# The first product of three of four MLP blocks as seven half-size products, with the masks loaded once per mixer

## The chip, the core and the metric

The kernel runs on one core of one Trainium2 chip. TensorE multiplies, VectorE (DVE), ScalarE (ACT) and GpSimd (POOL) work element by element, and SyncE (SP) issues nearly all transfers between the chip's memory and the core. The metric is the device time of one execution in microseconds (us); less is better.

## What is computed

The reference runs one step of a two-layer decoder. Each layer has a mixer (recurrent heads, different in layer 0 and layer 1) and an MLP, both followed by a layer norm:

```python
h = _layer_norm(ALPHA * h + mixed, p['ln1_g'][layer], p['ln1_b'][layer])
h = _layer_norm(ALPHA * h + _sq_relu_mlp(h, p['mlp_w1'][layer], p['mlp_w2'][layer]), ...)

def _sq_relu_mlp(h, w1, w2):
    return jnp.square(jax.nn.relu(h @ w1)) @ w2
```

There are 592 tokens (576 in the last MLP), the width is 1024 and the MLP is 4096 wide. All is fp32.

## The kernel before

Activations lie with the features on the 128 partitions and the tokens along the row: `H` is eight tiles of 128 features by 592 tokens. Every fp32 operand of a product is kept as two fp32r parts, a rounded copy made by ACT and the rest made by DVE (`split`, `parts`), and a product is three matmuls, high by high, high by low and low by high. The weights come as 252 units of 128 by 1024 through three `raw` buffers. `parts` splits a unit with one ACT cast (L126) and one DVE subtraction (L127) into one of five `w` buffers. A conventional tile (`mm`, L182) takes eight k-steps of three matmuls for each half of the tokens, so two tiles cost 96 matmuls of 296 tokens (288 in the last MLP).

The MLP works in four blocks of 1024 features. For a block the first product, w1, gives eight tiles; relu and square follow on ACT, and DVE and ACT split the squares into operands. The second product, w2, adds eight tiles into the running sums `r`. For three of the four blocks (`FAST`) w2 runs as pairs of tiles, and a pair takes seven products of half size in place of eight (`fast_pair`, `product` L195): four k-steps by three matmuls by seven are 84 matmuls. For that, DVE forms sums and differences of weights (L141, L142, L148, L149) and of squares (L632 to L638), and three and a half unit splits take the place of two. w1 is conventional in all four blocks, and so is w2 in the last one.

At the head of both mixers stands a small product with 16 columns of weights (`wsr`, 32 columns with the two parts; `mm32` L247 and `together` L311). Its weights for both layers are loaded and split once, while the input x arrives (L356 to L358). A table of masks (`msk`, 561 KB) is loaded once as well (L362). After layer 0 the output of the MLP is stored to memory for the residual of layer 1: eight times a POOL addition (L682) and a store issued by POOL (L683). These are the last things that read the `r` tiles.

The order of the instructions on each engine is fixed when the program is built. A scheduler takes the code in the order in which it is written and moves instructions past each other by costs of its own; where a buffer is taken over from an earlier tile, it puts in waits for all that used that tile. An engine then runs its list in order.

Of the kernel before, what the change touches and what calls it, by code (L numbers as in the profile page):

```python
# [14 lines left out]
P = 128  # L15
# [56 lines left out]
def _trunk(ctx, tc, nc, I, O):  # L72
# [20 lines left out]
    msk = const.tile([P, NMSK], F32, name="msk")  # L93
# [3 lines left out]
    onesr = const.tile([P, P], F32R, name="onesr")  # L97
# [5 lines left out]
    def mk(name):  # L103
        a, b = MSK[name]
        return msk[:, a:b]

    ident, umask, lsmask, uxmask, lxmask, seqm, sel, blk = (
        mk(n) for n in ("ident", "u", "ls", "ux", "lx", "seq", "sel", "blk"))
# [95 lines left out]
    def fast_pair(xs, n, y11, y12, y21, y22):  # L204
# [5 lines left out]
        def add(y, p):  # L210
            V.tensor_tensor(y, y, p[:, :n], OP.add)  # L211

        def sub(y, p):
            V.tensor_tensor(y, y, p[:, :n], OP.subtract)
# [4 lines left out]
        add(y11, X)  # L219
        product(W, u1, HD, xs["b21"], n, True)  # L220
        add(y11, W)
        flush()
        prep_to(base + 5)
        product(Z, u3, HD, xs["t1"], n, True)
        sub(y22, Z)
# [3 lines left out]
        add(y12, X)  # L229
        product(Z, u2, HD, xs["b22"], n, False)  # L230
        add(y12, Z)
# [3 lines left out]
        sub(y22, X)  # L235

        def rest():
            product(X, u4, 0, xs["t4"], n, False)
            sub(y21, X)
# [106 lines left out]
    with ExitStack() as st:  # L346
# [15 lines left out]
    nc.sync.dma_start(msk, I["msk"])  # L362
    nc.sync.dma_start(row, I["row"])
    G.memset(ones, 1.0)
    A.copy(onesr, ones)
# [218 lines left out]
    def mlp(H, layer, halves, last, keep=None):  # L584

        n = halves[0][1] - halves[0][0]
        c0, c1 = halves[0][0], halves[1][1]
        with ExitStack() as st:
            rp = pool("mr", KT, stack=st)
            tp = pool("mt", 1, stack=st)  # L590
            fp = pool("mf", 5, stack=st)
            rs = [rp.tile([P, T], F32, tag="r", name="r") for _ in range(KT)]
            ff, stage, made = {}, {}, {}
            out = [None]
            scratch = []

            def new(name):
                if not scratch:
                    scratch.append(fp.tile([P, 7, T], F32, tag="ff", name="ln"))
                    scratch.append(0)  # L600
                scratch[1] += 1
                return scratch[0][:, scratch[1] - 1]
# [926 lines left out]
def layout(inp):  # L1529
# [32 lines left out]
    def mlp_units(l):  # L1562
# [6 lines left out]
        for b in range(4):  # L1569
            if b < 3:  # L1570
                u += a(b + 1, 0, 2)
# [104 lines left out]
```

## Time and profile before

| | |
|---|---|
| time, median of three runs | 1898.5 us (1894.89 to 1899.44) |
| the profiled execution's own time | 1896.57 us |
| its span in the trace | 1894.8 us |
| TensorE (PE) busy | 1842.8 us, 97% of the span |
| DVE busy | 1258.0 us, 66% |
| ACT busy | 942.3 us, 50% |
| POOL busy | 363.4 us, 19% |

The trace gives each instruction's start and duration. On DVE and ACT the end of an instruction overlaps the start of the next, so what one costs in a full queue is the distance between two starts. The view of stretches gives for each engine how long it was busy between two times and PEclk, the share of TensorE's full clock that was granted: 1.00 is 2.4 GHz and 0.50 is 1.2 GHz. PE is the row of matmuls and PEld the row of weight loads beside it. Names are the program's tiles with the buffer numbers left out, and an arrow points from inputs to output.

### The profile page before, as it was taken

What the parts mean: (1) busy time and instruction counts of PE and PEld (TensorE: products, weight loads), DVE (VectorE), ACT (ScalarE), POOL (GpSimd) and SP (SyncE); (2) the same over time, 40 slices, a digit from 0 to 9 for tenths busy, and PEclk for the clock granted to TensorE, in tenths of its full rate; (3) what the DMA queues carried; (4) which work ended last, traced back from release to release, by engine and by line L of the source; (5) the groups of instructions that cost most, each with busy time, mean ns of one, the idle gap of its engine ahead of it and who ended that gap; (6) DMA issues with size and microseconds to landing.
All of it is one profiled execution on the core that took longest, in us unless ns stands there. A gap on an engine that the chain in (4) does not pass through costs nothing.

```text
span 1894.8 us, 33652 instructions
## 1 busy us (share of the span) xinstructions
PE 1842.8 (97%) x13822; PEld 1802.8 (95%) x13822; DVE 1258.0 (66%) x2003; ACT 942.3 (50%) x1718; POOL 363.4 (19%) x403
## 2 busy tenths in 40 slices
PE   8999999998999999998999999999999899999996
PEld 8998999998999999997999999999999899999996
DVE  7776757759875757458754565665755976666638
ACT  6656456624744443324644455666632653534333
POOL 2122324015000000145322121221203200000015
PEclk9999999999999999999999999999999999999998
DMA  6232221321222232313323233223231214141411
GB/s 220 91 115 72 88 101 68 114 84 56 67 80 99 67 112 68 120 59 113 113 96 114 104 103 104 80 99 106 82 128 57 78 57 134 45 134 45 134 57 50
DMA packets 68761, 175.96 MB, mean 93 GB/s; under 512 B 6624, under 2 KB 30304, under 8 KB 67456
## 3 DMA queue, kind: packets, MB, share of 16 engines
q1 hardware_dynamic: 67968, 171.40, 26.9%
q8 instruction: 108, 1.77, 0.4%
q0 software_dynamic: 640, 2.43, 0.3%
q14 instruction: 45, 0.37, 0.1%
HBM read 154.54 MB, written 19.25 MB: 92 GB/s over the span
## 4 chain that ended last, share of the span: by engine, by line
PE 81%; DVE 13%; ACT 3%; issue 2%; POOL 0%; DMA 0%; ACTq 0%; DVEq 0%
PE pm L182 54%; PE pm L195 14%; PE pm L311 2%; DVE w L127 2%; DVE r L515 1%; DVE r L531 1%; DVE h L533 1%; DVE r L451 1%; PE px L1375 1%; DVE acc L748 1%; PE px L1386 1%; PE px L1385 1%; PE px L1118 1%; ACT w L126 1%; PE px L1314 1%
## 5 line engine op out<-in xcount | busy, mean ns | idle before, releaser
L182 PE MATMUL pm<-h,w 128*128 128x296 f32 (+2 forms) x7728 | 1102.1, 301 | 6.2 <-ACT h L334 5.6
L182 PEld LDWEIGHTS pm<-h,w 128*128 128x128 f32 x7728 | 1057.6, 189 | 16.1 <-ACT h L334 5.6
L127 DVE TENSOR_TENSOR w<-raw,w 128x1024 fp32r<-128x1024 f32 (+1 forms) x300 | 367.3, 1225 | 199.0 <-ACT w L126 197.8
L126 ACT CAST w<-raw 128x1024 fp32r<-128x1024 f32 (+1 forms) x300 | 304.1, 1014 | 293.2 <-PE pm L195 153.1
L195 PE MATMUL pm<-ff,w 128*128 128x296 f32 (+1 forms) x2016 | 273.3, 297 | 0.0
L195 PEld LDWEIGHTS pm<-ff,w 128*128 128x128 f32 x2016 | 272.0, 188 | 0.0
L657 POOL TENSOR_TENSOR sq<-sq 128x296 f32<-128x296 f32 (+1 forms) x32 | 21.5, 674 | 652.4 <-ACT sq L655 652.4
L182 PE MATMUL pm<-m,w 128*128 128x296 f32 (+1 forms) x768 | 105.1, 298 | 0.0
L182 PE MATMUL pm<-ff,w 128*128 128x296 f32 (+1 forms) x768 | 105.0, 298 | 0.0
L182 PEld LDWEIGHTS pm<-m,w 128*128 128x128 f32 x768 | 103.8, 188 | 0.4
L182 PEld LDWEIGHTS pm<-ff,w 128*128 128x128 f32 x768 | 103.7, 188 | 0.4
L311 PE MATMUL pm<-h,w 128*128 128x296 f32 (+1 forms) x528 | 82.7, 314 | 13.7 <-DVE r L556 6.5
L311 PEld LDWEIGHTS pm<-h,w 128*128 128x128 f32 x528 | 77.5, 200 | 18.2 <-ACT h L532 12.2
L644 DVE TENSOR_TENSOR ff<-sq,ff 128x888 fp32r<-128x888 f32 (+3 forms) x48 | 58.6, 1221 | 41.1 <-ACT ff L643 41.0
L625 ACT ACTIVATE sq<-pm 128x296 f32<-128x296 f32 (+1 forms) x96 | 37.4, 414 | 88.0 <-PE pm L182 66.3
L643 ACT CAST ff<-sq 128x888 fp32r<-128x888 f32 (+3 forms) x48 | 50.4, 1050 | 37.9 <-DVE sq L638 37.2
L1410 POOL TENSOR_TENSOR o<-o,zs 128x576 f32<-128x576 f32 x16 | 30.8, 1935 | 152.0 <-DVE o L1409 152.0
L211 DVE TENSOR_TENSOR r<-r,pm 128x296 f32<-128x296 f32 (+1 forms) x96 | 43.5, 453 | 18.8 <-PE pm L195 18.1
L1329 POOL TENSOR_TENSOR sin<-sin,ebl 128x1024 f32<-128x1024 f32 (+1 forms) x12 | 31.2, 2597 | 97.9 <-issue 93.1
L655 ACT ACTIVATE sq<-pm 128x296 f32<-128x296 f32 (+1 forms) x32 | 13.0, 414 | 56.8 <-PE pm L182 53.8
L626 ACT ACTIVATE sq<-sq 128x296 f32<-128x296 f32 (+1 forms) x96 | 40.7, 450 | 0.8
L1415 ACT COPY v<-pm 128x296 f32<-128x296 f32 x32 | 12.9, 406 | 56.7 <-PE pm L182 56.7
(392 smaller groups left out, 2248.0 us busy)
## 6 DMA issues: line engine op xcount, KB each, us to landing
raw<-in_w_dram SPq DMA_DIRECT2D x252, 512.0 KB, 3.3
sin<-in_sst_dram SPq DMA_DIRECT2D x8, 512.0 KB, 3.3
out_ssd_s_dram<-sin SPq DMA_DIRECT2D x8, 512.0 KB, 3.2
sin<-in_gst_dram SPq DMA_DIRECT2D x4, 1024.0 KB, 6.5
out_gla_s_dram<-sin SPq DMA_DIRECT2D x4, 1024.0 KB, 3.9
sin<-in_hst_dram SPq DMA_DIRECT2D x8, 512.0 KB, 4.2
out_hgrn_s_dram<-sin SPq DMA_DIRECT2D x8, 512.0 KB, 3.5
xt<-in_x_dram SPq DMA_DIRECT2D x16, 148.0 KB, 3.7
```

The costliest lines, as they stand in the source:

```text
L126: A.copy(w[:, 0, :n], r)
L127: V.tensor_tensor(w[:, 1, :n], r, w[:, 0, :n].bitcast(F32), OP.subtract)
L182: PE.matmul(p[:, :n], w[:, a, ks], xs[k][:, b, c0:c1], start=(k == 0 and i == 0), stop=(k == KT - 1 and i == 2))
L195: PE.matmul(p[:, :n], w[:, a, ks], xs[k][:, b, :n], start=(first and k == 0 and i == 0), stop=(k == 3 and i == 2), skip_group_check=True)
L211: V.tensor_tensor(y, y, p[:, :n], OP.add)
L311: PE.matmul(o[:, :c1 - c0], w, t.xs[k][:, b, c0:c1], start=(k == 0 and j == 0), stop=(k == KT - 1 and j == len(ops) - 1))
L625: A.activation(q, p, AF.Relu)
L626: A.activation(q, q, AF.Square)
L643: A.copy(t[:, 0, a:e, :n], s[:, a + 1:e + 1, :n])
L644: V.tensor_tensor(t[:, 1, a:e, :n], s[:, a + 1:e + 1, :n], t[:, 0, a:e, :n].bitcast(F32), OP.subtract)
L1329: G.tensor_tensor(sin, sin, ebl[:, 0:8].unsqueeze(2).to_broadcast([P, 8, N]), OP.mult)
L1410: G.tensor_tensor(o[v][:, c], o[v][:, c], gate[v][:, c], OP.mult)
```

## The change

**w1.** Block 0 keeps its conventional w1. In blocks 1 to 3 the eight tiles are four pairs of seven products (`w1_pair`). Six of the seven activation operands are formed once per MLP: `operands`, behind each of the last four tiles of block 0, forms three differences per pair of input tiles and splits them; `last_operand`, behind each of the first four w2 pairs, forms a fourth in place of a part of `H`. A w1 pair moves partial sums from PSUM with ACT copies and DVE additions, since they are squared afterwards and not added to `r`. The matmuls of the whole program go from 13103 to 12815.

**Buffers.** Four buffers hold the squares (five before); `stage` takes every second scratch tile from them.

**Masks.** `msk` and the small weights leave the fixed area. `masks` takes memory for them at the start of each mixer, loads the whole table and the 16 columns of that layer, and splits these. In both mixers that memory is the one at byte 109728 of a partition. In layer 0 it held the input tiles and then the scratch of the start-up arithmetic; in layer 1 it held the `r` tiles 0, 7 and 3 of the MLP before (the table takes the bytes of 0 and 7, the small weights those of 7 and 3).

```diff
-    wsm = const.tile([P, 2, KT, 16], F32, name="wsm")
-    wsr = const.tile([P, 2, KT, 32], F32R, name="wsr")
...
+    def masks(stack, layer):
...
+        sp = pool("mskp", stack=stack)
+        t = sp.tile([P, NMSK], F32, name="msk")
+        nc.sync.dma_start(t, I["msk"])
+        small = sp.tile([P, KT, 32], F32R, name="wsr")
+        r = sp.tile([P, KT, 16], F32, name="wsm")
+        nc.sync.dma_start(r, I["wsm"][:, layer])
+        A.copy(small[:, :, 0:16], r)
+        V.tensor_tensor(small[:, :, 16:32], r, small[:, :, 0:16].bitcast(F32), OP.subtract)
...
-        nc.sync.dma_start(wsm, I["wsm"])
-        A.copy(wsr[:, :, :, 0:16], wsm)
-        V.tensor_tensor(wsr[:, :, :, 16:32], wsm, wsr[:, :, :, 0:16].bitcast(F32), OP.subtract)
...
-    nc.sync.dma_start(msk, I["msk"])
...
-            fp = pool("mf", 5, stack=st)
+            fp = pool("mf", 4, stack=st)
...
+            def operands(i):
+
+                for k in (i, i + 4):
+                    h = H[k][:, :, c0:c1].bitcast(F32)
+                    V.tensor_tensor(rs[k][:, c0:c1], h[:, 0], h[:, 1], OP.add)
...
+                V.tensor_tensor(x[:, 0], rs[i][:, lo], rs[i][:, hi], OP.subtract)
+                V.tensor_tensor(x[:, 1], rs[i + 4][:, hi], rs[i][:, hi], OP.subtract)
+                V.scalar_tensor_tensor(x[:, 2], rs[i + 4][:, hi], -1.0, x[:, 0], OP.mult, OP.subtract)
+                split_to(t[:, :, :, :n], x)
...
+                def w0(px_, pw):
+                    nonlocal s
+                    s = Squares(b, i)
+                    A.copy(s.x(0, 0), px_)
+                    V.tensor_tensor(s.x(0, 0), s.x(0, 0), pw, OP.add)
+                    s.done(0, 0)
...
+            for b in range(FAST):
+                for j in range(0, KT, 2):
+                    w2_pair(b, j)
+                    if b == 0:
+                        last_operand(j // 2)
+                for i in range(4):
+                    w1_pair(b + 1, i)
+            flush()
...
-        run([conv[0], Task(H, FULL, dt_consume, small=wsr[:, 0]), conv[1]], by_half=True)
+        run([conv[0], Task(H, FULL, dt_consume, small=mk("small")), conv[1]], by_half=True)
...
     with ExitStack() as st:
+        mk = masks(st, 1)
         gp = pool("go", NGO, stack=st)
```

Where the change moves instructions, three places are shown. `raw` and `w` are a weight unit and its split, `xt` and `h` the input and its split, `lbt` and `e01` small tables of the start-up arithmetic, `res` the stored residual.

**The start, DVE, before.** The small weights are split right behind the first half of the input.

```order
L335 TENSOR_TENSOR h_86<-xt_102,h_86 128x296 [waits DMAHW7_49,Activation_49]
L335 TENSOR_TENSOR h_87<-xt_103,h_87 128x296 [waits DMAHW0_49,Activation_49]
L358 TENSOR_TENSOR wsr_77<-wsm_76,wsr_77 128x16x16 [waits DMAHW1_49,Activation_49]
L391 TENSOR_SCALAR hcw_166<-vec_73 128x48 [waits DMAHW3_49]
L392 TENSOR_SCALAR hcb_167<-vec_73 128x12
```

**The start, DVE, after.** The same split now stands behind the second half of the input, the splits of the next three weight units and all of the start-up arithmetic.

```order
L420 TENSOR_TENSOR e01_194<-e01_194 128x8 [waits DVE_49]
L422 TENSOR_TENSOR lbt_162<-e01_194 128x8 [waits DVE_49]
L423 TENSOR_SCALAR lbt_162<-lbt_162 128x8 [waits DVE_49]
L424 TENSOR_TENSOR lbt_162<-lbt_162 128x8 [waits DVE_49]
L108 TENSOR_TENSOR wsr_214<-wsm_215,wsr_214 128x8x16 [waits DMAHW6_49,Activation_49]
L128 TENSOR_TENSOR w_475<-raw_473,w_475 128x1024 [waits DMAHW2_49,PE_49,Activation_49]
```

The split has moved from tenth to forty-sixth place on DVE; on PE the small product keeps its place as the second product of the program.

**The start, SP, after.** The load of the small weights stood tenth and that of the table twenty-first; now all of the first eight weight units are issued ahead of them.

```order
L121 DMA raw_473<-in_w_dram 128x1024 [waits DMAHW6_49,DMAHW2_49,DVE_49]
L121 DMA raw_546<-in_w_dram 128x1024 [waits DMAHW7_49,DMAHW3_49,DVE_49]
L121 DMA raw_645<-in_w_dram 128x1024 [waits DMAHW4_49,DMAHW0_49,DVE_49]
L103 DMA msk_212<-in_msk_dram 128x1122 [waits DMAHW5_49,DVE_49,Activation_49]
L106 DMA wsm_215<-in_wsm_dram 128x128
```

They stand thirtieth and thirty-first. The value of DVE's counter that the load of the table waits for is the one that `lbt` (L422) sets, since scratch of that arithmetic lay in the table's memory.

**The head of layer 1, SP, before and after.** First before:

```order
L1177 DMA wg2_9453<-in_wg2_dram 32x512 [waits PE_49]
L1179 DMA rmask_9455<-in_rmask_dram 128x592
L1181 DMA cmask_9457<-in_cmk_dram 128x192
L1210 DMA sin_9817<-in_gst_dram 128x2048 [waits DVE_49,PE_49,Activation_49]
L120 DMA raw_9893<-in_w_dram 128x1024 [waits DMAHW4_49,DVE_49]
```

And now:

```order
L121 DMA raw_9739<-in_w_dram 128x1024 [waits DMAHW2_49,DVE_49,Activation_49]
L121 DMA raw_9933<-in_w_dram 128x1024 [waits DMAHW3_49,DVE_49,Activation_49]
L1290 DMA sin_9978<-in_gst_dram 128x2048 [waits Pool_49]
L103 DMA msk_9596<-in_msk_dram 128x1122 [waits DMASW7_49,DMASW0_49,Pool_49]
L106 DMA wsm_9599<-in_wsm_dram 128x128 [waits DMAHW4_49,DMASW3_49]
L121 DMA raw_10054<-in_w_dram 128x1024 [waits DMAHW5_49,DVE_49]
```

The eight stores of the residual count on the semaphores DMASW0 to DMASW7, one each, so the load of the table waits for the stores of the tiles 0 and 7, and the load of the small weights stands behind it on SP.

**The end of layer 0, POOL, after.** These are the last additions and stores of the residual:

```order
L756 TENSOR_SCALAR r_5391<-r_5391,vec_73 128x592 [waits DVE_49]
L756 TENSOR_SCALAR r_5392<-r_5392,vec_73 128x592 [waits DVE_49]
L757 DMA res_5372<-r_5391 128x592 [waits Pool_49]
L757 DMA res_5372<-r_5392 128x592 [waits Pool_49]
L1306 TENSOR_TENSOR e4_9987<-ls_9865 128x16 [waits DVE_49,PE_49]
```

`r_5392` is tile 7, and its store is the eighth and last. Only four memsets of the mixer, which stood behind the stores, have moved ahead of them.

**The MLP, DVE.** Before, one pair of w1 tiles of block 1 (four tile halves):

```order
L632 TENSOR_TENSOR sq_6653<-sq_6653 128x296
L127 TENSOR_TENSOR w_6753<-raw_6751,w_6753 128x1024
L644 TENSOR_TENSOR ff_6656<-sq_6653,ff_6656 128x888
L127 TENSOR_TENSOR w_6817<-raw_6813,w_6817 128x1024
L636 TENSOR_TENSOR sq_6653<-sq_6653 128x296
L637 SCALAR_TENSOR_TENSOR sq_6653<-sq_6653 128x296
L638 SCALAR_TENSOR_TENSOR sq_6653<-sq_6653 128x296
L644 TENSOR_TENSOR ff_6656<-sq_6653,ff_6656 128x1184
```

Now, the first twelve of the seventeen rows from one pair's first addition to the next pair's:

```order
L716 TENSOR_TENSOR sq_6614<-sq_6614,pm_6559 128x296
L128 TENSOR_TENSOR w_6611<-raw_6607,w_6611 128x1024
L623 TENSOR_TENSOR ff_6480<-sq_6479,ff_6480 128x888
L692 SCALAR_TENSOR_TENSOR sq_6479<-sq_6479 128x296
L623 TENSOR_TENSOR ff_6480<-sq_6479,ff_6480 128x296
L623 TENSOR_TENSOR ff_6480<-sq_6479,ff_6480 128x592
L128 TENSOR_TENSOR w_6633<-raw_6609,w_6633 128x512
L623 TENSOR_TENSOR ff_6615<-sq_6614,ff_6615 128x296
L142 TENSOR_TENSOR raw_6609<-raw_6609 128x512
L720 TENSOR_TENSOR sq_6614<-sq_6614,pm_6560 128x296
L143 TENSOR_TENSOR raw_6609<-raw_6609,raw_6607 128x512
L149 TENSOR_TENSOR raw_6607<-raw_6607,raw_6609 128x512
```

DVE holds three and a half unit splits and four sums of weights per pair where two unit splits stood, and three additions out of PSUM that were not there.

## Rows read from the trace of the kernel before

**Rows 1.** Page, part 1: busy us (share of the span) and instructions.

```profile
PE 1842.8 (97%) x13822; PEld 1802.8 (95%) x13822; DVE 1258.0 (66%) x2003; ACT 942.3 (50%) x1718; POOL 363.4 (19%) x403
```

**Rows 2.** Chain that ended last: start us, us, engine, tile, line, count.

```profile
630.06 44.25 PE pm L195 x324
...
1647.41 43.02 PE pm L195 x324
```

**Rows 3.** Stretches: us, busy of PE, PEld, DVE, ACT, POOL, PEclk, DMA share, GB/s.

```profile
300.00:362.00 62.00, 59.43 (x398) 57.26 (x397) 53.77 (x86) 38.77 (x74) 19.08 (x23) 0.97 0.35 112
458.00:493.00 35.00, 30.29 (x202) 29.14 (x201) 30.79 (x54) 21.50 (x45) 6.99 (x7) 0.95 0.23 75
630.00:676.00 46.00, 46.00 (x339) 46.00 (x338) 37.66 (x59) 17.39 (x19) 0.00 (x0) 1.00 0.28 93
```

**Rows 4.** DVE in order of time in a w2 pair: start us, us, line.

```profile
640.11 1.22 DVE L127 TENSOR_TENSOR w<-raw,w 128x1024 fp32r<-128x1024 f32 x1
641.25 0.45 DVE L214 TENSOR_TENSOR r<-r,pm 128x296 f32<-128x296 f32 x1
641.62 1.21 DVE L127 TENSOR_TENSOR w<-raw,w 128x1024 fp32r<-128x1024 f32 x1
...
646.88 0.69 DVE L141 TENSOR_TENSOR raw<-raw 128x512 f32<-128x512 f32 x1
647.60 0.69 DVE L142 TENSOR_TENSOR raw<-raw 128x512 f32<-128x512 f32 x1
648.21 0.45 DVE L211 TENSOR_TENSOR r<-r,pm 128x296 f32<-128x296 f32 x1
```

**Rows 5.** DVE groups in the w1 stretch: count, busy us, mean ns, idle before.

```profile
L644 DVE TENSOR_TENSOR ff<-sq,ff 128x888 fp32r<-128x888 f32 x3 | 3.2, 1081 | 3.7 <-ACT ff L643 3.7
```

**Rows 6.** The start in order of time: start us, us, engine, line, idle before.

```profile
9.36 0.41 DVE L358 TENSOR_TENSOR wsr<-wsm,wsr 128x256 fp32r<-128x256 f32 x1
11.61 2.28 PE L247 MATMUL pm<-h,wsr 128*32 128x296 f32 x16
13.17 3.12 DVE L335 TENSOR_TENSOR h<-xt,h 128x296 fp32r<-128x296 f32 x8
18.94 0.97 DVE L379 SCALAR_TENSOR_TENSOR spt<-spt 128x8 f32<-128x8 f32 x5 [1.60 <-POOL spt L377]
```

**Rows 7.** Issue to landing: the table, then the small weights, at the start.

```profile
DMA to landing us min/median/max: 5.1/5.1/5.1
DMA to landing us min/median/max: 3.3/3.3/3.3
```

**Rows 8.** Stretches at the start, columns as in rows 3.

```profile
11.60:26.00 14.40, 14.40 (x108) 13.44 (x105) 10.23 (x31) 9.93 (x29) 2.51 (x10) 1.00 0.79 274
```

**Rows 9.** End of layer 0, head of layer 1, in order of time.

```profile
869.26 0.43 PE L311 MATMUL pm<-h,wsr 128*32 128x296 f32 x2
...
884.65 0.43 PE L311 MATMUL pm<-h,wsr 128*32 128x296 f32 x2
...
886.12 0.44 PE L311 MATMUL pm<-h,wsr 128*32 128x296 f32 x2
...
889.06 3.46 PE L182 MATMUL pm<-h,w 128*128 128x296 f32 x24
...
892.88 0.33 SPq L1210 DMA_DIRECT2D sin<-in_gst_dram  x1
...
905.99 1.13 POOL L683 DMA_DIRECT2D res<-r  x2
```

**Rows 10.** Issue to landing of the eight stores of the residual.

```profile
DMA to landing us min/median/max: 2.4/3.6/5.0
```

**Rows 11.** Stretches at the head of layer 1, columns as in rows 3.

```profile
873.00:874.00 1.00, 0.00 (x0) 0.00 (x0) 1.00 (x4) 0.46 (x2) 0.00 (x0) 0.89 0.00 0
874.00:875.00 1.00, 0.53 (x2) 0.56 (x3) 1.00 (x4) 0.86 (x3) 0.54 (x1) 0.50 0.00 0
879.00:880.00 1.00, 1.00 (x5) 0.75 (x4) 0.00 (x0) 0.51 (x2) 0.00 (x0) 0.50 0.74 242
```

More of the change, by code (lines that the diff above doesn't have):

```diff
@@ L101, in vc @@
         return vec[:, o:o + n]
[L103 to L108, printed above, removed]
+    def masks(stack, layer):
[7 more added lines that the diff above has]
+        V.tensor_tensor(small[:, :, 16:32], r, small[:, :, 0:16].bitcast(F32), OP.subtract)
+        return lambda name: small if name == "small" else t[:, slice(*MSK[name])]
     prepped = {}
@@ L208, in fast_pair, with take, w0, z0 @@
         X, W, Z = pm(), pm(), pm()
[L210 to L214, printed above, removed]
+        def take(m, *ps):
+            if m in got:
+                got[m](*(p[:, :n] for p in ps))
+        def w0():
+            product(W, u1, HD, xs["b21"], n, True)
+            flush()
+            prep_to(base + 5)
+            take("w0", *((W,) if sums else (X, W)))
+        def z0():
+            product(Z, u3, HD, xs["t1"], n, True)
+            take("z0", Z)
         prep_to(base + 4)
@@ L218, in fast_pair @@
         product(X, u1, 0, xs["b11"], n, True)
[L219 to L225, printed above, removed]
+        take("x0", X)
+        if sums:
+            flush()
+            prep_to(base + 5)
+            z0()
+            w0()
+        else:
+            w0()
+            z0()
         weave()
@@ L611, in w1, with stage, split_to @@
-            def w1(b, f):
+                    tst.close()
+                    t = pool("mn", 1, stack=st).tile([P, 7, T], F32, name="ln")
+                    scratch.extend(t[:, k] for k in range(7))
+                return scratch.pop()
+            def stage(i=1):
+                return (sp if i % 2 else fp).tile([P, 5, CS], F32, tag="ms" if i % 2 else "ff", name="sq")
+            norm = Norm(new, rs, halves, "ln2g", "ln2b", layer, last)
+            def split_to(t, x):
+                A.copy(t[:, 0], x)
+                V.tensor_tensor(t[:, 1], x, t[:, 0].bitcast(F32), OP.subtract)
@@ L660, in w1, with w1_pair, z1, x2 @@
-                return Task(H, halves, squares if b < FAST else plain)
+                        made[i] = Squares(0, i)
+                    made[i].done(g, half, p)
+                return Task(H, halves, consume)
+            def w1_pair(b, i):
+                xs = {"b11": [H[k][:, :, lo] for k in range(4)], "b21": [H[k][:, :, lo] for k in range(4, 8)],
+                      "b22": [H[k][:, :, hi] for k in range(4, 8)], "t4": [H[k][:, :, hi] for k in range(4)]}
+                for o, m in enumerate(("t1", "t3", "t2")):
+                    xs[m] = [turned[k][:, :, o] for k in range(4)]
+                s = None
+                def w0(px_, pw):
[4 more added lines that the diff above has]
+                    s.done(0, 0)
+                def z1(p):
+                    V.tensor_tensor(s.x(0, 1), s.x(0, 1), p, OP.add)
+                    s.done(0, 1)
+                def x2(p):
+                    V.tensor_tensor(s.x(1, 1), s.x(1, 1), p, OP.add)
+                    s.done(1, 1, scale=-1.0)
+                fast_pair(xs, n, {"w0": w0, "z0": lambda p: A.copy(s.x(1, 1), p), "x1": lambda p: A.copy(s.x(0, 1), p),
+                                  "z1": z1, "x2": x2, "x3": lambda p: s.done(1, 0, p, -1.0)}, False)
```

186 lines of the change are left out of this document (96 added, 90 removed).

## The prediction

> **What bounds the kernel now.** I read the page's busy times first [rows 1]: TensorE is busy 97% of the span, DVE 66% and ACT 50%. So matmuls that go away shorten the run, as long as nothing else takes over the place where they stood. Next come the chain of waits and the stretches of the MLP [rows 2, 3]. In both the matmuls follow each other without a gap, and a w2 pair stage (630 to 676) has PE busy for all of its 46.00 us with DVE at 37.66. The reader should see two things. PE sets the time in the MLP, and DVE, which the change loads further, is already at 82% where products of half size run. Last I read the places where PE stands still, the start and the head of layer 1 [rows 6, 9], because the order there is changed.
>
> **What goes.** The program loses 13103 - 12815 = 288 matmuls, half in each MLP: 12 pairs of tiles by 96 - 84. A matmul of 296 tokens costs 44.25/324 = 0.1366 us and one of 288 tokens 43.02/324 = 0.1328 us [rows 2]. That is 144 x 0.1366 + 144 x 0.1328 = 19.7 + 19.1 = **38.8 us**, all of it on PE's path.
>
> **What DVE gets in the MLP.** I price DVE by the distance between starts [rows 4]: a unit split of 1024 takes 641.25 - 640.11 = 1.14, an operation on 296 0.37, and a sum of 512 weights 0.72 where the next one depends on it and 0.61 where not. A w1 pair needs three splits of 1024 (3.4), one of 512 (0.6), four sums (2.7), three additions from PSUM (1.1), four differences of squares (1.6) and splits of 888, 592 and twice 296. The one of 888 lasts 1.08 [rows 5], so about 1.0 between starts; that of 592 is some 0.7 by its size and the two small ones are 0.7, in all 2.4. The sum is 11.8 us. PE's share is 84 x 0.1366 = 11.5. In blocks 1 and 2 DVE thus has slightly more to do than PE. In the w2 pairs of block 0 the fourth operand adds four operations, 1.6, to the 37.66/4 = 9.4 of now, which makes 11.0 of 11.5. The other w2 pairs and the w1 pairs of block 3, whose squares go through POOL, keep slack. So in each MLP some 12 pairs, 138 us, run with DVE at 95 to 103%.
>
> The trace has no such stretch in the MLP. Sheer work gives the lower bound, 8 pairs x 0.3 = 2.6 us per MLP, 5 for both. The dearest near row is 458 to 493, with DVE at 30.79/35 = 88% and PE without work for 4.7 of 35 us, 13%: 18.5 per MLP, 37 for both, and as DVE is fuller here I put the upper end at 45. The nearest in kind is 300 to 362, DVE at 87%, where PE loses 2.6 of 62, 4% [rows 3]: 5.7 per MLP. A gain below nothing is excluded, since the matmuls already stand back to back. Each of the three passages from w1 to w2 per MLP adds a chain (addition, relu, square, cast, subtraction) of about as much as the 12 matmuls that cover it. I take **25 us** for both MLPs, between the two rows, because both had a DVE less full than this one will be. `operands` and the ACT copies lie in block 0 and on an ACT that is free half of the time; with that cover gone they are inside the same 25.
>
> **What the masks cost at the start.** Now `wsr` is ready at 9.36 + 0.41 = 9.8 and the small product, second in PE's order, runs at 11.61 [rows 6]. From there PE is busy for 14.40 of 14.40 us [rows 8], and everything in that stretch stands behind the small product. In the new order the table's load waits for `lbt` on DVE. The second half of the input is split by 13.17 + 3.12 = 16.3 [rows 6]. Behind it come the first of three casts and its hand-over (1.4), three subtractions (3 x 1.14), eight dependent start-up steps of 0.2 (five take 0.97) and ten more of 0.17 with a trip to ACT (2.3): 16.3 + 1.4 + 3.4 + 1.6 + 2.3 = 25.0. Then SP issues the table and the weights, 0.4 each (an issue on SP takes 0.33 in [rows 9]), and the landing takes 3.3 for the weights, behind a table that took 5.1 [rows 7]; I take 4, so 29.8. The cast and the subtraction, 0.4 each [rows 6], give 30.5. PE stands from 11.6 to 30.5, 18.9 us, with nothing that it may run. On top comes the clock. After an idle stretch the granted share was 0.50, the lower level of 1.2 GHz, from 874 to 880 with PE at work [rows 11], which halves some 5 us of matmuls: 2 to 3 us. Together **21 us**. The bounds are 15, if `lbt` comes right behind the third weight unit, and 24, if the weights too take 5.1.
>
> **What they cost at the head of layer 1.** Here the table takes memory that was last read by the eighth store of the residual, and the small weights stand behind it on SP. The last two stores are issued from 905.99 on, 1.13 for both, so the eighth at 906.6 [rows 9]. Landing took 2.4 to 5.0, median 3.6 [rows 10]: 910.2. Two issues on SP (0.8), the landing of the weights behind the table (3.3), the cast and the subtraction (0.8) bring the first small matmul to 915. At present it runs at 869.26, and the work behind it is done while the norm of the second half still runs. That work at full clock is eight groups at 886.12 - 884.65 = 1.47, or 11.8, and then what runs from 889.06 to 908.0, 18.9 [rows 9]. From 915 it ends at 945.7 in place of 908.0, which is 37.7 later, with 2 to 3 for the clock again: **40 us**. The bounds are 36 and 45, from the earliest and the latest landing and a chain of additions that might start a microsecond or two sooner, since no matmuls disturb the norm. Behind all this PE is busy without a gap, so nothing is given back. Queued behind the waiting split on DVE and the cast on ACT is only work on PE's results, and behind the loads on SP are weight units that have no free buffer yet.
>
> The store is also where the skill speaks. The Trainium skill, "DMA: Bandwidth & Descriptors", section "Anatomy of one DMA — SWDGE (gpsimd) path", says that the semaphore fires only when the last byte is confirmed in the target memory, about 2.0 us fixed plus bytes at 436 GB/s. As an estimate from that page a store of 303 KB takes 2.7 us. By it the sum would be 0.9 lower; the median of the eight stores says 3.6, and I keep that.
>
> **The sum.** Against the profiled execution's own 1896.57: 1896.6 - 38.8 + 25 + 21 + 40 = 1943.8, rounded to **1943 us**. The median of the three runs, 1898.5, lies 1.9 above the profiled one, well inside the range. A difference below 0.3%, 5.7 us, cannot be told from no change.
>
> **The rivals.**
> - *The loads of the masks are hidden.* Then both stalls go and 1896.6 - 38.8 + 25 = 1883 is left, faster. The place is the two small products, the price 61 us together, and the run breaks even where no more than 38.8 - 25 = 14 us of it is paid. For it speaks that either load takes only 3.3 to 5.1 us [rows 7] and SP is mostly idle. Against it speak the order, which puts `lbt` and the eighth store ahead of the loads, and POOL's row at 905.99 [rows 9]: the stores would have to land some 30 us sooner.
> - *DVE takes the whole gain of the MLP.* If the fuller DVE costs PE 50 us or more, as at 458 to 493 [rows 3] but over the whole of blocks 0 to 2, the time is 1896.6 - 38.8 + 50 + 61 = 1969 or more. Against it speaks 300 to 362, which had the same DVE load and lost a third of that.
> - *DVE costs nothing.* PE stays back to back as in the w2 pairs now [rows 3]: 1896.6 - 38.8 + 61 = 1919. This lies in the range.
> - *The change does not do what it says.* The built program has 288 matmuls less, so only the order of the rest could defeat it; I leave 1% for that.
>
> **How the numbers follow.** My forecast, both stalls in full and a part of the MLP's gain lost, has 75%, and 1915 (38.8 saved, 15, 36 and 5 paid) to 1968 (24, 40 and 45 paid, with a microsecond or two off) are its ends. DVE taking all has 11%, stalls shorter than my bounds but still a slower kernel (1903 to 1915) 6%, hidden loads 7% and the last rival 1%. The 7% for hidden loads divide into 4 for faster and 3 for the same, with the 1% among the slower. So the chances are 0.04 faster, 0.03 within 0.3%, 0.93 slower, and the range 1915 to 1968 leaves out about 2 in 10.
>
> **What would show it.** In the new profile PE should stand idle from about 12 to 30 us and from about 882 less the first MLP's gain to some 33 us later, both times ended by the subtraction that makes `wsr` (L108), with a granted clock of 0.50 behind each. The w1 pairs of blocks 1 and 2 should have DVE above 90% and take 46 to 50 us per block in place of 49 now, with short waits of PE for DVE or ACT. If PE starts within 5 us of its present time at either head, or if DVE has idle time in those pairs while PE waits, the step is wrong.

## The result: 1940.5 us, 2.3% slower

Four runs of the changed kernel gave a median of 1940.47 us (1939.35 to 1941.1), four of the kernel before 1897.47 (1894.89 to 1899.44). The ratio is 1.0227, with a 95% interval from 1.0209 to 1.0244. The forecast was 1943, within 1915 to 1968. The profiled execution took 1940.13 us with a span of 1938.4.

Busy us, share of the span and instructions of each engine, after the change (before: [rows 1]):

```profile
PE 1820.5 (94%) x13534; PEld 1766.0 (91%) x13534; DVE 1411.8 (73%) x2332; ACT 1020.7 (53%) x1903; POOL 370.2 (19%) x403
```

The 288 matmuls are gone (13822 - 13534), and PE is busy for 22 us less in a longer span, 94% where it was 97%. DVE has 154 us more. The three longest entries of the list of waits of PE (engine, tile and line that waited, releaser, us in total, times, longest) name where PE stands now; the first two did not exist before:

```profile
PE pm L324 <- DVE wsr L108: 33.2, 1, 33.2
PE pm L260 <- DVE wsr L108: 18.7, 1, 18.7
PE px L508 <- DVE ln L479: 12.5, 4, 8.0
```

To see what each part of the program takes, I use one landmark: the first matmul of the norm's shift (tile `lnc` or `ln`, L448 before and L456 after), which comes four times. The rows are the timeline of PE, before and then after: start us, us, engine, line, tiles, count.

```profile
424.03 1.16 PE L448 MATMUL px<-lnc,ones 128*128 128x296 f32 x4
...
835.31 1.16 PE L448 MATMUL px<-ln,ones 128*128 128x296 f32 x4
...
1446.04 1.13 PE L448 MATMUL px<-lnc,ones 128*128 128x288 f32 x4
...
1847.26 1.13 PE L448 MATMUL px<-ln,ones 128*128 128x288 f32 x4
```

```profile
445.22 1.26 PE L456 MATMUL px<-lnc,ones 128*128 128x296 f32 x4
...
847.15 1.16 PE L456 MATMUL px<-ln,ones 128*128 128x296 f32 x4
...
1494.64 1.13 PE L456 MATMUL px<-lnc,ones 128*128 128x288 f32 x4
...
1890.90 1.16 PE L456 MATMUL px<-ln,ones 128*128 128x288 f32 x4
```

The differences of these rows give the stages. The last rows of the table are experiments told of below; all are from the profiled execution of each.

| kernel | start and mixer 0, to the first norm | MLP 0 | head and mixer 1 | MLP 1 | time, median |
|---|---|---|---|---|---|
| before | 424.0 | 411.3 | 610.7 | 401.2 | 1897.5 |
| after | 445.2 | 401.9 | 647.5 | 396.3 | 1940.5 |
| difference | +21.2 | -9.4 | +36.8 | -5.0 | +43.0 |
| forecast | +21 | -19.7 + 12.5 | +40 | -19.1 + 12.5 | +47.2 |
| start_early | 423.0 | 400.4 | 648.2 | 397.4 | 1918.2 |
| head_free | 446.3 | 401.7 | 619.4 | 397.6 | 1913.8 |
| both_free | 423.5 | 400.6 | 617.8 | 398.5 | 1889.7 |
| split_early | 424.8 | 401.4 | 609.4 | 398.4 | 1880.7 |
| masks_alone | 445.0 | 412.9 | 645.0 | 401.3 | 1956.6 |
| small_late | 450.3 | 399.4 | 636.1 | 397.3 | 1933.9 |
| stores_first | 446.1 | 402.2 | 643.0 | 397.3 | 1937.6 |
| no_sums | 422.3 | 399.8 | 610.4 | 389.9 | 1871.5 |
| no_operands | 422.7 | 396.0 | 609.4 | 392.2 | 1870.0 |
| neither | 422.6 | 395.3 | 609.4 | 388.0 | 1865.0 |
| pool_split | 422.6 | 420.8 | 610.4 | 412.1 | 1915.0 |

**The start.** PE in order of time, after (the kernel before ran the small product at 11.61, [rows 6]):

```profile
7.06 6.03 PE L183 MATMUL pm<-h,w 128*128 128x296 f32 x23 [0.68 <-DVE h L348]
31.82 4.16 PE L260 MATMUL pm<-h,wsr 128*32 128x296 f32 x16 [18.72 <-DVE wsr L108]
35.77 7.21 PE L183 MATMUL pm<-h,w 128*128 128x296 f32 x48
```

The idle time ahead of the small product is 18.72 us and ended by the subtraction that makes `wsr`. SP's own rows show that the loads were issued only when the start-up arithmetic had reached `lbt` (L422, done at 26.2), 26.25 for the table and 26.62 for the weights:

```profile
26.25 0.33 SPq L103 DMA_DIRECT2D msk<-in_msk_dram  x1
26.62 0.42 SPq L106 DMA_DIRECT2D wsm<-in_wsm_dram  x1
```

And the stretches show the clock: 1.2 GHz (0.50) for the first 4.2 us of work after the idle time, full clock from 38 on.

```profile
31.80:36.00 4.20, 4.18 (x17) 3.04 (x18) 0.00 (x0) 0.00 (x0) 0.00 (x0) 0.50 0.00 0
...
38.00:50.00 12.00, 12.00 (x90) 11.38 (x89) 4.06 (x7) 4.78 (x10) 0.58 (x3) 1.00 0.14 45
```

**The head of layer 1.** PE again: after the last matmuls of the MLP it waits twice, 8.05 us for the sums of the norm's second half and 33.20 us for `wsr`.

```profile
867.36 13.80 PE L183 MATMUL pm<-ff,w 128*128 128x296 f32 x99
889.21 1.33 PE L508 MATMUL px<-ln,ones 128*128 128x296 f32 x2 [8.05 <-DVE ln L479]
...
925.18 0.70 PE L324 MATMUL pm<-h,wsr 128*32 128x296 f32 x2 [33.20 <-DVE wsr L108]
```

The last two stores on POOL, then the two loads on SP, then the cast on ACT:

```profile
916.97 1.13 POOL L757 DMA_DIRECT2D res<-r  x2
```

```profile
920.48 0.33 SPq L103 DMA_DIRECT2D msk<-in_msk_dram  x1
920.92 0.36 SPq L106 DMA_DIRECT2D wsm<-in_wsm_dram  x1
```

```profile
924.51 0.30 ACT L107 CAST wsr<-wsm 128x128 fp32r<-128x128 f32 x1 [20.46 <-DMA wsm<-in_wsm_dram]
```

The chain of waits has the landings between them, the eighth store's and the weights':

```profile
917.56 2.82 DMA res<-r
...
920.92 3.49 DMA wsm<-in_wsm_dram
```

The store is issued at 917.56 and lands 2.82 us later, the table's load follows at 920.48, and the weights land 3.49 us after their issue at 920.92. In the stretches PE is idle for 33 us and then works at 0.50 until about 930:

```profile
892.00:925.00 33.00, 0.00 (x0) 0.00 (x0) 13.34 (x22) 5.01 (x11) 23.05 (x20) 0.50 0.41 151
...
926.00:928.00 2.00, 2.00 (x10) 1.92 (x10) 0.00 (x0) 0.00 (x0) 0.00 (x0) 0.50 0.00 0
...
930.00:932.00 2.00, 2.00 (x12) 1.85 (x12) 0.00 (x0) 0.00 (x0) 0.00 (x0) 0.72 0.00 0
```

**The MLPs.** The stretches of block 0's w2 pairs, which begin at 541 (548 to 588), block 1's w1 pairs (588 to 635), the passage to its w2 pairs (635 to 650) and these (650 to 682), then the same passage in the second MLP (1670 to 1694). The columns are those of [rows 3].

```profile
548.00:560.00 12.00, 11.01 (x76) 9.96 (x74) 12.00 (x23) 7.55 (x10) 0.00 (x0) 1.00 0.13 45
560.00:588.00 28.00, 27.85 (x201) 27.38 (x202) 27.10 (x50) 8.78 (x13) 0.00 (x0) 1.00 0.29 95
588.00:635.00 47.00, 46.70 (x342) 46.32 (x342) 44.81 (x73) 35.84 (x69) 0.00 (x0) 1.00 0.28 90
635.00:650.00 15.00, 14.30 (x96) 13.03 (x96) 14.47 (x26) 8.67 (x14) 0.00 (x0) 1.00 0.22 72
650.00:682.00 32.00, 32.00 (x233) 31.74 (x234) 27.43 (x44) 10.70 (x12) 0.00 (x0) 1.00 0.31 100
...
1670.00:1694.00 24.00, 22.68 (x155) 20.49 (x153) 22.35 (x39) 15.09 (x28) 0.00 (x0) 1.00 0.27 88
```

DVE is busy for 95 to 100% from 548 to 650, where before it was at 82% in a w2 stage [rows 3] and, between 588 and 635, nearly all of it w1, at 26.58 of 47 us:

```profile
588.00:635.00 47.00, 47.00 (x347) 47.00 (x346) 26.58 (x36) 25.08 (x43) 0.00 (x0) 1.00 0.17 56
```

Yet in the w1 pairs themselves PE loses only 0.3 of 47 us. It loses where w1 gives way to w2, there and in the first microseconds behind: the counts of matmuls show it better than the busy times, 76 in the 12 us from 548 to 560 and 96 in the 15 us from 635 to 650, where 88 and 110 would fit at 0.1366 us each.

### The profile page after: what moved, and what is told of

Same layout as the page of the kernel before. It is cut to its first block, busy times and chain, and to the rows that moved or that the text cites. A ratio compares the mean times of both kernels' runs of the same rounds, so it can differ in the third digit from the quotient of the medians.

```text
span 1938.4 us, 33527 instructions
## 1 busy us (share of the span) xinstructions
PE 1820.5 (94%) x13534; PEld 1766.0 (91%) x13534; DVE 1411.8 (73%) x2332; ACT 1020.7 (53%) x1903; POOL 370.2 (19%) x403
## 4 chain that ended last, share of the span: by engine, by line
PE 68%; DVE 17%; ACT 6%; issue 4%; POOL 2%; DMA 2%; SPq 0%; ACTq 0%; DVEq 0%; POOLq 0%
PE pm L183 37%; PE pm L196 18%; PE pm L324 3%; DVE w L128 3%; ACT w L127 2%; DVE r L523 1%; POOL sq L675 1%; DVE r L459 1%; PE px L1455 1%; DVE h L541 1%; DVE r L539 1%; POOL r L756 1%; ACT sq L671 1%; DVE acc L824 1%; PE px L1466 1%
## 5 line engine op out<-in xcount | busy, mean ns | idle before, releaser
L183 PE MATMUL pm<-h,w 128*128 128x296 f32 (+2 forms) x5424 | 790.6, 302 | 6.4 <-ACT h L347 5.8
L183 PEld LDWEIGHTS pm<-h,w 128*128 128x128 f32 x5424 | 746.8, 189 | 16.7 <-ACT h L347 5.8
L128 DVE TENSOR_TENSOR w<-raw,w 128x1024 fp32r<-128x1024 f32 x348 | 412.1, 1186 | 136.5 <-ACT w L127 134.6
L127 ACT CAST w<-raw 128x1024 fp32r<-128x1024 f32 x348 | 342.8, 989 | 311.6 <-PE pm L183 110.6
L196 PE MATMUL pm<-h,w 128*128 128x296 f32 (+1 forms) x1152 | 166.1, 298 | 1.8 <-DVE sq L724 0.9
L196 PEld LDWEIGHTS pm<-h,w 128*128 128x128 f32 x1152 | 158.0, 188 | 4.6 <-ACT sq L727 2.4
L196 PE MATMUL pm<-t,w 128*128 128x296 f32 (+1 forms) x864 | 124.5, 297 | 1.0 <-ACT sq L727 0.7
L196 PEld LDWEIGHTS pm<-t,w 128*128 128x128 f32 x864 | 118.5, 188 | 1.7 <-ACT sq L727 1.2
L324 PE MATMUL pm<-h,w 128*128 128x296 f32 (+1 forms) x528 | 81.7, 311 | 9.4 <-DVE r L564 6.7
L324 PEld LDWEIGHTS pm<-h,w 128*128 128x128 f32 x528 | 77.0, 198 | 12.2 <-ACT h L540 7.3
L736 DVE TENSOR_TENSOR r<-r,pm 128x296 f32<-128x296 f32 (+1 forms) x168 | 74.9, 452 | 11.2 <-PE pm L196 10.5
L622 ACT CAST ff<-sq 128x296 fp32r<-128x296 f32 (+5 forms) x96 | 58.0, 618 | 24.4 <-DVE sq L692 11.6
L623 DVE TENSOR_TENSOR ff<-sq,ff 128x296 fp32r<-128x296 f32 (+5 forms) x96 | 64.4, 685 | 5.1 <-ACT ff L622 4.5
```

Of the source, the lines that this page charges most:

```text
L127: A.copy(w[:, 0, :n], r)
L128: V.tensor_tensor(w[:, 1, :n], r, w[:, 0, :n].bitcast(F32), OP.subtract)
L183: PE.matmul(p[:, :n], w[:, a, ks], xs[k][:, b, c0:c1], start=(k == 0 and i == 0), stop=(k == KT - 1 and i == 2))
L196: PE.matmul(p[:, :n], w[:, a, ks], xs[k][:, b, :n], start=(first and k == 0 and i == 0), stop=(k == 3 and i == 2), skip_group_check=True)
L324: PE.matmul(o[:, :c1 - c0], w, t.xs[k][:, b, c0:c1], start=(k == 0 and j == 0), stop=(k == KT - 1 and j == len(ops) - 1))
L622: A.copy(t[:, 0], x)
```

## The experiments

The runs come in several sets. The kernel before, run again in each, had medians from 1896.8 to 1898.6 us, so a difference of up to 2 us between kernels of different sets is not told from none by the medians alone.

**start_early: the start undone alone.** The masks of layer 0 lie beside the input tiles, and their loads stand where they stood before.

```diff
     H = new_h()
     prep_to(1)
+    early = ExitStack()
+    mk, table, weights = masks(early, 0, True)
...
         load(*FULL[0])
+        weights()
         prep_to(2)
         nc.sync.dma_start(vec, I["vec"])
         load(*FULL[1])
+    table()
```

> Only the start is undone: the masks of layer 0 get memory beside the input tiles, the small weights are loaded and split behind the first half of the input and the table behind the second half, as in the kernel before; layer 1 keeps the changed form. My theory (the place of the load behind the start-up arithmetic is the whole cost there, 21.3 us by the first additions of the first norm, 425.75 before and 447.05 after): 1940.5 - 21 = 1919 us, the second product at about 11.6 us again. Rival (the loads are late for another reason, or the mixer behind them had slack that takes the gain): over 1930 us.

Measured: 1918.19 us, 22.3 less than after. The first stage fell from 445.2 to 423.0, all others stayed within 1.6. The place of the load is the whole cost of the start, and nothing behind it takes the gain back.

**head_free: another memory at the head of layer 1.**

```diff
-        mk = masks(st, 1)
         gp = pool("go", NGO, stack=st)
+        mk = masks(st, 1)
```

> Only the head of layer 1 is changed: the masks are allocated behind the 26 activation tiles in place of ahead of them, so that their memory is that of old square operands and not of residual tiles; the same loads, splits and products. My theory (the wait for the eighth residual store is the whole cost there, 36.8 us between the first additions of the norm of layer 0 and the first masked product of layer 1): 1940.5 - 37 = 1903.5 us, with the first small product right behind the first half of the norm. Rival (the activation tiles, which now take the memory of the first residual tile, wait for the stores in its place): only half of it comes back, 1920 us or more.

Measured: 1913.82 us, 26.7 less and not 37, between the two expectations. The rival's reason does not show: PE has no wait here that an activation tile ends. Its rows show what is left:

```profile
868.14 13.80 PE L183 MATMUL pm<-ff,w 128*128 128x296 f32 x99
889.98 1.33 PE L508 MATMUL px<-ln,ones 128*128 128x296 f32 x2 [8.04 <-DVE ln L479]
...
896.40 0.70 PE L324 MATMUL pm<-h,wsr 128*32 128x296 f32 x2 [3.64 <-DVE wsr L108]
```

It stands still for 8.04 us ahead of the norm's products of the second half (L508, L510) and 3.64 more ahead of the small product. On DVE the subtraction of `wsr` stands behind the second half's own subtractions (L523), though its load, issued at 881.65, had landed within 4.7 us:

```profile
893.86 1.68 DVE L523 TENSOR_TENSOR r<-r,ln 128x296 f32<-128x296 f32 x2
895.46 0.89 DVE L108 TENSOR_TENSOR wsr<-wsm,wsr 128x128 fp32r<-128x128 f32 x1
```

Before, the first small product ran at 869.26 [rows 9], ahead of the second half's sums, which are L500 there:

```profile
878.26 1.19 PE L500 MATMUL px<-ln,ones 128*128 128x296 f32 x2
```

So a second cause lies under the first: the split of the small weights is written with the mixer, behind the whole norm, and the scheduler puts it late on DVE and ACT, and the small product behind L508 and L510 on PE. The run split_early, below, takes this place away.

**both_free: both of these together**, the two diffs above.

> Both of the above together; the MLP stays as changed. If the two stalls are independent and all that the masks cost, the gains add: 1940.5 - 21 - 37 = 1882 us, 15 below the kernel before, which is what 288 matmuls less (38.8 us) leave after 24 us lost inside the MLPs. Rival (the start and the head take time from each other or from the MLP, or the MLP loses more without the idle time ahead of it): 1890 to 1905 us.

Measured: 1889.66 us, ratio to before 0.9963 (0.995 to 0.9976). The gains add: 22.3 + 26.7 = 49.0, measured 50.8. The 8 us missing against the expectation are those of the head.

**masks_alone: the mask part of the change on the kernel before.** `masks` and its calls as in the diff of the change, everything else as before.

```diff
-    msk = const.tile([P, NMSK], F32, name="msk")
-    wsm = const.tile([P, 2, KT, 16], F32, name="wsm")
-    wsr = const.tile([P, 2, KT, 32], F32R, name="wsr")
...
+        mk = masks(st, 0)
         gp = pool("ge", NGE, stack=st)
...
+        mk = masks(st, 1)
         gp = pool("go", NGO, stack=st)
```

> The kernel before with the mask part of the change alone: the masks and small weights in memory taken at the head of each mixer, as in the changed kernel, and the MLP as it was, with 13103 matmuls. My theory (masks cost 21 at the start and 37 at the head of layer 1, whatever the MLP does): 1897.5 + 58 = 1955 us. Rival (a part of the idle time at the head of layer 1 comes from the new MLP, whose residual tiles are finished in another order): 1897.5 + 21 + less than 25, 1940 us or less.

Measured: 1956.56 us, 59.4 above before: 21.0 at the start, 34.3 at the head, 1.6 in MLP 0 in the profiled execution, which took 1953.39, 3.2 less than the median. The idle time is the masks' own and needs nothing of the new MLP. The new MLP then gives 1956.6 - 1940.5 = 16 us back.

**split_early: the split at the head of layer 1 ahead of the norm.** To both_free it adds that the masks of layer 1 are taken, loaded and split where the norm of layer 0's MLP begins, at the upper end of the memory, which the operand sets `t` have left by then.

```diff
-        sp = pool("mskp", stack=stack)
+        sp = pool("mskp", stack=stack, side="right" if layer else "left")
...
                     t = pool("mn", 1, stack=st).tile([P, 7, T], F32, name="ln")
+                    if layer == 0:
+                        top.append(masks(right, 1))
```

> As both_free, but the masks of layer 1 are loaded and split when the norm that ends layer 0 begins, into memory at the top that the operand sets of w1 have left. In head_free PE stood still for 8.0 us ahead of the norm's products for the second half and 3.6 us more for the split of the small weights, which on DVE and ACT stands behind the norm of the second half, because the code of the mixer is written behind it. My theory: that place in the order, and not the memory, is what is left of the cost at the head; 1889.7 - 8 to 11 = 1879 to 1882 us. Rival (the 10 us left come from the residual stores or from the new MLP's tail): 1887 us or more.

Measured: 1880.65 us, 9.0 below both_free and the fastest of the kernels that leave nothing out: ratio to before 0.9918 (0.9904 to 0.9933). The stage of the head is 609.4, that of before 610.7. The small product now stands ahead of the second half's sums again, as the timeline of PE shows:

```profile
860.02 0.43 PE L336 MATMUL pm<-h,wsr 128*32 128x296 f32 x2
...
869.31 0.66 PE L524 MATMUL px<-ln,ones 128*128 128x296 f32 x2
```

**no_sums: less DVE work in the w1 pairs.** In `last` and `sums1` of the w1 pairs the four additions are left out.

```diff
-            V.tensor_tensor(a22, a21, a22, OP.add)
-            V.tensor_tensor(a21, a21, n, OP.add)
+            if sums:
+                V.tensor_tensor(a22, a21, a22, OP.add)
+                V.tensor_tensor(a21, a21, n, OP.add)
```

> split_early without the four sums of weights of each w1 pair (w1 is then not multiplied by the right sums; the work of all other engines and the products stay): 2.7 us of 11.8 less on DVE in 12 pairs of each MLP. If DVE's load in and behind the w1 pairs makes PE lose 10 us in the first MLP and 14 in the second, most of that goes: 8 to 18 us below split_early. Rival (the loss at the passages from w1 to w2 is the latency of the chain from the last square to the operand, or the wait for one of four buffers): less than 4 us below it.

Measured: 1871.54 us, 9.1 less than split_early: 1.6 in MLP 0, 8.5 in MLP 1 by the profiled executions. (That of split_early took 1883.17 us, 2.5 above its median, most of it in the first stage.) That the second MLP gains more fits its smaller PE share (a matmul of 288 tokens in place of 296, while the weights cost DVE the same), but no run here shows that this is the reason.

**no_operands: less DVE work in block 0.**

```diff
-                x = stage()[:, 0:3, :n]
-                V.tensor_tensor(x[:, 0], rs[i][:, lo], rs[i][:, hi], OP.subtract)
...
-                split_to(t[:, :, :, :n], x)
+                A.copy(t[:, 0, 0:2, :n], rs[i][:, c0:c1].rearrange("p (h c) -> p h c", c=n))
+                A.copy(t[:, 0, 2, :n], rs[i + 4][:, lo])
+                G.memset(t[:, 1].bitcast(F32), 0.0)
```

> split_early without the differences and splits of the first activation operands in block 0 (ACT copies and zeros from POOL stand in their place, so w1 of blocks 1 to 3 is not right): about 2.3 us less on DVE for each of the four tiles, once per MLP. If the loss at the first passage (2.9 us in the first MLP, and as much in the second) comes from that work on a full DVE, 4 to 7 us below split_early in all. Rival (that passage is as slow as the later ones, whoever fills DVE): within 2 us of it.

Measured: 1869.99 us, 10.7 less than split_early, 5.4 and 6.2 in the two MLPs; I had expected 4 to 7 in all. The first passage is healed, as PE's rows show. First split_early, whose 324 matmuls of block 0's w2 pairs stretch from 520.18 to the next product at 567.4, with short waits for DVE's additions and a weight split:

```profile
520.18 10.22 PE L208 MATMUL pm<-ff,w 128*128 128x296 f32 x72
530.63 3.91 PE L208 MATMUL pm<-ff,w 128*128 128x296 f32 x26 [0.22 <-DVE r L754]
534.86 1.62 PE L208 MATMUL pm<-ff,w 128*128 128x296 f32 x10 [0.33 <-DVE w L140]
536.83 9.05 PE L208 MATMUL pm<-ff,w 128*128 128x296 f32 x60 [0.35 <-DVE r L754]
546.05 21.50 PE L208 MATMUL pm<-ff,w 128*128 128x296 f32 x156 [0.16 <-ACT w L139]
```

Then no_operands, where they run in one piece, 44.46 us, near the 44.25 of [rows 2]:

```profile
516.86 44.46 PE L208 MATMUL pm<-ff,w 128*128 128x296 f32 x324
```

That is some 3 of the 5.4 us of this MLP; the rest is spread over other stretches. The edit also leaves out the scratch tile that the differences take (`stage`), so the run prices the operands as a whole and not DVE's time alone.

**neither: both left out**, the two diffs above.

> split_early without the sums of weights of the w1 pairs and without the first activation operands of block 0, both of the above left out (so w1 of blocks 1 to 3 is not right). If DVE's load is the whole of what the MLPs lose against 288 matmuls less (about 26 us by split_early: 401.4 and 398.4 us in place of 391.6 and 382.1), the two gains of 9.1 and 10.7 add, 1880.7 - 20 = 1861 us. Rival (both took away the same stall at the passage behind them): 1867 to 1870 us, no better than the better one.

Measured: 1864.99 us, 15.7 less than split_early, between the two expectations: the gains overlap by some 2 to 4 us (the kernel before was 1.8 slower in this set). Against what 288 matmuls less would leave (411.3 - 19.7 and 401.2 - 19.1), the MLPs still lose 3.7 and 5.9 us.

**pool_split: a weight split per pair on POOL.**

```diff
         def plain():
             r.extend((load_unit(u), load_unit(u + 1)))
-            return parts(r[0])
+            return parts(r[0], G)
```

> split_early with one of the weight splits of each pair (the first, which is needed latest) made by POOL, which stands idle in the MLP, in place of DVE: 1.14 us of 11.0 to 11.8 less on DVE per pair. If only the count of DVE's work matters, 5 to 10 us below split_early, 1871 to 1876. Rival (POOL's work makes DVE's slower while it runs, as at the norm, where subtractions of 296 columns last 1.0 to 1.1 us on DVE beside POOL and 0.45 without): DVE gains nothing, since POOL needs 3 us for it, and the time is that of split_early or up to 20 us above.

Measured: 1915.04 us, 34.4 above split_early and beyond even the rival's range. Both MLPs are longer, by 19.4 and 13.7. One split on POOL, and what DVE did meanwhile:

```profile
564.87 2.40 POOL L140 TENSOR_TENSOR w<-raw,w 128x1024 fp32r<-128x1024 f32 x1 [10.22 <-ACT w L139]
```

```profile
564.94 2.65 DVE L663 TENSOR_TENSOR sq<-t,h 128x296 f32<-128x296 f32 x1
567.63 0.47 DVE L664 TENSOR_TENSOR sq<-sq,t 128x296 f32<-128x296 f32 x1
```

A sum of 296 columns, both inputs in on-chip memory, that lasts 0.45 us elsewhere started 0.07 after POOL's split and lasted 2.65: it ended 0.3 after POOL did. Beside POOL's next split (577.37 to 579.77) an addition that takes one input from PSUM (L734) kept its 0.46, and a weight split of 512 columns lasted 1.84 in place of 0.68:

```profile
577.63 0.46 DVE L734 TENSOR_TENSOR sq<-sq,pm 128x296 f32<-128x296 f32 x1 [0.69 <-ACT sq L733]
...
578.49 1.84 DVE L140 TENSOR_TENSOR w<-raw,w 128x512 fp32r<-128x512 f32 x1
```

So the work went from one engine to both. PE itself waits for a split of POOL's only once in each MLP (1.9 us each); its longest waits are for ACT's copies out of PSUM (L745), 17.1 us in all where split_early has 1.1. What held those copies up was not taken apart, so the path from the slower DVE to the 34.4 us stays open. The Trainium skill, "GPSIMD Engine Reference", section "1. Specifications", says that this engine shares its memory interfaces with VectorE and contends with instructions that read two inputs from there; the trace agrees, and 2.65 in place of 0.45 us is its price here.

**small_late: another order at the two heads of the changed kernel.**

```diff
-        run([conv[0], Task(H, FULL, dt_consume, small=mk("small")), conv[1]], by_half=True)
+        run([conv[0], conv[1], Task(H, FULL, dt_consume, small=mk("small"))], by_half=True)
...
-                ts = [Task(H, FULL, lr_consume, small=mk("small"))] + tasks
+                ts = tasks + [Task(H, FULL, lr_consume, small=mk("small"))]
```

> The changed kernel, with its masks and waits as they are, but the small product is written behind the others at both heads: behind the second weight product in layer 0 and behind all four in layer 1. If PE stands still only because the small product is the next in its list, it can now run 24 matmuls ahead of it at the start (3 to 5 us) and 192 at the head of layer 1 (26 us), so 1940.5 - 30 = 1910 us. Rival (what stands behind also waits for the stores or the masks, or the results of the small product are then missed later): 1925 us or more.

Measured: 1933.86 us, 6.6 less and not 30. My number for the head was too high, because the order runs the first halves of all four products, then the small one, then the second halves: 96 matmuls pass the wait and not 192.

```profile
894.49 8.91 PE L324 MATMUL pm<-h,w 128*128 128x296 f32 x63
928.12 3.57 PE L260 MATMUL pm<-h,wsr 128*32 128x296 f32 x16 [24.73 <-DVE wsr L108]
```

PE still waits 24.73 us, and the product comes at 928.12 (925.18 after): the end of the wait is set by the load, and order only fills it. The head gained 11.4, and the start lost 5.0, since the results of the small product now come too late for the recurrence behind it (PE waited 8.6 us for L1038's states, 2.4 after).

**stores_first: the order of the residual stores in the changed kernel.**

```diff
-                    for k in range(KT):
+                    for k in (0, 7, 3, 1, 2, 4, 5, 6):
                         G.tensor_scalar(rs[k], rs[k], vc("ln2b", layer * 8 + k), None, OP.add)
```

> The changed kernel with the residual stores in the order 0, 7, 3, 1, 2, 4, 5, 6, so that the tiles whose memory the masks take are stored earlier; the scheduler puts tile 7 fifth in POOL's list, where it was eighth. If the wait for the eighth store ends the idle time at the head of layer 1, the small product comes two or three stores sooner, 4 to 6 us: 1940.5 - 5 = 1935 us. Rival (the wait ends with the load itself or its place on SP): 1939 us or more.

Measured: 1937.59 us, 2.9 less; the stage of the head is 4.5 shorter. Tile 7's store stands fifth now, and SP issues the table at 916.11, 4.4 us sooner than after, though this kernel's norm began 1.1 us later:

```profile
916.11 0.33 SPq L103 DMA_DIRECT2D msk<-in_msk_dram  x1
```

By the median this lies between the two expectations and is little more than the sets differ. SP's row decides it: the load moved with the store, so the store of tile 7 does end its wait.

## Why the prediction was right, and where it was not

**The sum.** 38.8 saved, 25 + 21 + 40 paid, 1943; measured 1940.5. The two stalls came within 10% of their stages, and the 25 within 3% of what the MLPs lost, if the 38.8 is right. Four slips changed nothing: the terms add up to 1943.8, which was written as 1943; four operations of 0.37 are 1.5 and not 1.6; the upper end of the range takes 40 for one of two terms that were each bounded at 45; and the chances outside the range add up to 25 in 100, not 2 in 10.

**38.8 for 288 matmuls.** The count is exact, but no run here is free of loss in the MLPs, so the 38.8 itself is still a product of count and duration. The nearest, neither, has MLPs shorter by 16.0 and 13.2, 29.2 together.

**21 at the start.** Measured 21.2 by the stage, and 22.3 when start_early undid it. Step by step the table's load was issued at 26.25 (the prediction's sum gave 25.0 for the end of the arithmetic), and the small product ran at 31.82 and not 30.5. That the weights landed 4.3 us after their issue, and not 4, is the smaller part of it: ACT casts two parts of the table (L840, L841) from 30.74 on, when the table has landed, and the weights behind them at 31.14. PE waited 18.72 (forecast 18.9), and the clock of 0.50 stood behind it for some 5 us.

**40 at the head of layer 1.** Measured 36.8. The time of the small product was right: 915 on the old time axis, which the start and the first MLP move by 847.15 - 835.31 = 11.8, so 926.8 against 925.18. The store landed in 2.82 us, where I took the median of 3.6; in the changed kernel all eight landed in 2.4 to 2.8, median 2.7. The estimate from the Trainium skill ("DMA: Bandwidth & Descriptors", "Anatomy of one DMA — SWDGE (gpsimd) path"), 2.7, was the nearer one here. What failed is the step from the wait to its price. I put all 40 on the wait for the eighth store, and only 26.7 come back when that wait goes (head_free). The other 9 to 10 are the place of the split in DVE's list and of the small product in PE's, behind the second half of the norm (split_early, -9.0). The order of the changed kernel has these rows on DVE and PE; the prediction drew only on those of SP and POOL. The rival of hidden loads had the right end all the same: with both waits gone and the split in its old place the kernel takes 1880.7, where the rival said 1883. The text's place of the idle stretch ("882 less the first MLP's gain") left out the 21 us of the start; it began at 892.0.

**25 in the MLPs.** Measured 19.7 - 9.4 = 10.3 and 19.1 - 5.0 = 14.1, together 24.4. The size was right, the make-up was not, and that the two misses cancel is luck. Of the 10.3 in the first MLP only 3.5 are idle time in PE's row (9.7 us in that stage, 6.2 before); the rest is busy time in which fewer matmuls ran. Three things differ:
- I took 12.5 for each MLP, by the prices of 296 columns. In MLP 1 PE's part of a w1 pair is 84 x 0.1328 = 11.2 and DVE's weights cost the same; this fits its larger loss, 14.1 against 10.3, and was not tested by itself.
- `operands` and the copies I had put "inside the same 25" at no price of their own. They are the largest piece that was taken away, 10.7 for both MLPs (no_operands), and part of it lies where they fill DVE, at the passage to block 0's w2 pairs; the four sums of a w1 pair are the next, 9.1 (no_sums).
- In the stretches shown the loss does not lie in the w1 pairs, where DVE is at 95% and PE loses 0.3 of 47 us, but behind them, where DVE's backlog meets a chain that PE waits for. Of the 26.1 us that split_early loses in its MLPs, 16.5 go with those two pieces of DVE work (neither, by the stages; 15.7 by the medians). For the other 9.6 I have no experiment: the chain of addition, relu, square, cast and subtraction at each passage, the wait for one of four buffers and the rest of DVE's load are all left, and it stays open which of them it is.

**The signs.** PE stood idle from 13.1 to 31.8 and from 892.0 to 925.2, both times until the subtraction of `wsr`, with the clock at 0.50 behind each, and the w1 pairs of block 1 took 47 us with DVE at 95%, all as said.

**The rivals.** Hidden loads: shown wrong for the changed kernel, and right in its price for one that hides them. DVE taking the whole gain: wrong, 14.4 of 38.8 are left. DVE costing nothing: wrong by 24.4. The change doing what it says: 13534 matrix instructions against 13822.

## What to carry to other kernels

A table that is moved from a fixed place into reused memory brings along every wait of the tiles that lay there and the place in the program at which it is written; before moving it, look up who read those bytes last, and where each engine's list then has the load, the split and the first reader. Of two causes on one wait only the later one shows in the profile, so what a wait costs is known when it has been taken away, not when it has been read. And a matmul saved is worth its time only where the engine that pays for it has slack: here an engine at 95% cost nothing by itself, but its backlog at the next change of stage did, as far as the experiments reach.

## What the runs showed of the hardware

- A subtraction of 1024 columns with two inputs took POOL 2.40 us (DVE 1.21), and a DVE sum of 296 columns with both inputs in on-chip memory beside it 2.65 in place of 0.45, while an addition with one input from PSUM kept its 0.46. I had expected a slower DVE, 1.0 to 1.1 as beside POOL's work at the norm, and not one that stands until POOL has finished.
- After 33 idle us PE worked at the lower clock for some 5 us (granted 0.50 from 925 to 930, 0.72 from 930 to 932), after 18.7 idle us for 4.2 us and a little more.
- A store of 303 KB issued by POOL landed in 2.82 us as the last of eight; the eight together ranged from 2.4 to 2.8 in the changed kernel and from 2.4 to 5.0 in the kernel before [rows 10].
